# Two parts of x in one 512-column matmul: a float32 decoder trunk on one NeuronCore

## The chip, the cores and the metric

One core of one Trainium2 chip. The metric is the device time of one execution in microseconds (us), the median of three runs. TensorE (PE; its weight loads are shown as PEld), VectorE (DVE), ScalarE (ACT), GpSimd (POOL) and SyncE (SP) each work through a list of their own, in order, and wait for one another on semaphores.

## The reference

Two layers on 256 tokens of width 2048, all in float32:

```
h = rmsnorm(x, norm_mix[l])
x = x + (even_mixer if l == 0 else odd_mixer)(h)
h = rmsnorm(x, norm_ffn[l])
up = h @ w_up;  g, u = split(up)                 # 2 x 5632 columns
x = x + (silu(causal_dwconv(g, conv_w)) * u) @ w_down
...
return rmsnorm(x, norm_final)
```

The even mixer (layer 0) makes q, k, v, a and gate in one projection. Eight heads attend with three dilated windows; beside them a * sigmoid(gate) goes through a causal convolution of width 31, a LayerNorm and a swish. Both go through one output projection, the attention's 1024 rows and then the convolution's. The odd mixer (layer 1) is forgetting attention with 16 heads.

## The kernel before

**Split products.** Weights and activations are each split into two float32r parts whose sum is exact: hi (the rounded value) and lo (the rest). A product is hi·hi + hi·lo + lo·hi. The kernel reads 408 MB of weights once, each in panels of 512 output columns. `stream` (lines 79 to 98) brings 1 MB (four contraction tiles of 128 rows) into `raw` and splits it in two pieces of 128 x 1024: ACT casts `whi` (line 95), DVE subtracts `wlo` (line 96). There are three `raw` buffers and four of each part, so a cast waits until PE is done with the piece four before.

**`panel_b`** (lines 100 to 112) makes a feature-major product. For each of the panel's four feature tiles m it has one PSUM bank of 512 float32 columns, of which the 256 tokens fill the lower half, and for each contraction tile it issues three matmuls of 256 columns: whi with x's hi (line 109), whi with x's lo (line 110), wlo with x's hi (line 111). The weight is the stationary operand, so `whi` is loaded twice. I call these three a triple, and a matmul with its weight load a pass. There are five such banks. `panel_a` (lines 119 to 127) makes a token-major product: x is stationary, and the weight's 512 columns move, so all its passes are 512 columns wide (lines 115 to 117). It serves v in both layers and the last projection (names `acc_v`, `acc_d` of layer 1, `acc_e`).

**Who uses panel_b:** a and gate (`ag`, four panels), q and k of both layers, both output projections (`oa` for the attention's rows, `ob` for the convolution's, `oc` in layer 1), the forget gates (`fl`), the FFN's up projection (`g` and `u`, 11 panels each per layer) and layer 0's down projection (`d`). DVE evicts each bank with one instruction, mostly a multiplication by the norm's row or an addition to x (lines 293, 297, 377, 198, 462, 477, 516).

**What sets the order.** A scheduler writes each engine's list when the program is built, from its own estimate of durations and from priorities: splits of weights stand 400 steps ahead of their place, and the convolution's steps (`waiting`, lines 299 to 320) 300 behind it; a few of them are handed out behind each split (`pace`). What is left is handed out after `oa`'s second panel, and then comes `layer_norm` (lines 405 to 428), whose result y is `ob`'s moving operand: without it `ob` can't start. On the chip the lists are fixed.

Of the kernel before, what the change touches and what calls it, by code (L numbers as in the profile page):

```python
# [41 lines left out]
def trunk(ctx, tc, a):  # L42
# [25 lines left out]
    # work that may wait, traced a little at a time behind the weights' pieces  # L68
# [10 lines left out]
    def stream(src_of, nk, width, name, dk=4, room=None):  # L79
        """The split parts of a weight's panel, a few contraction tiles at a time."""  # L80
# [56 lines left out]
    xT = keep.tile([P, KT, T], F32, name="xT")  # L137
    xs_hi = keep.tile([P, KT, T], F32R, name="xs_hi")
    xs_lo = keep.tile([P, KT, T], F32R, name="xs_lo")
    xhi = lambda kt: xs_hi[:, kt, :]  # L140
    xlo = lambda kt: xs_lo[:, kt, :]
# [15 lines left out]
    def along_free(r, name):  # L157
        """A column per token [128, 2] as a row [128, T], the same on each partition."""
# [9 lines left out]
    def rstd_from(parts, n, name):  # L168
        """From partial sums [128, T] per partition: a column [128 tokens, 2] and a row [128, T]."""
# [21 lines left out]
    def finish_x(kt, gcol, ssq, name):  # L191
        """x's feature tile kt is complete: scaled split copy, and its squares."""
# [14 lines left out]
    ROWS = ((0, 0, P), (1, P, T))     # query tile, its columns in a head's scores, and its keys  # L207
# [34 lines left out]
    def weigh_v(pt, vt, h, yhi, ylo, kt, name):  # L242
# [4 lines left out]
        S.copy(yhi[:, kt, :], y[:, :T])  # L247
        V.tensor_tensor(out=ylo[:, kt, :], in0=y[:, :T], in1=yhi.bitcast(F32)[:, kt, :], op=ALU.subtract)

    # =====================================================================  # L250
    # Layer 0 mixer: dilated attention and Conformer convolution
    # =====================================================================
    with ExitStack() as ph:
# [15 lines left out]
        S.activation(dummy, ones[:, 0:1], AF.Copy)   # brings the activation table while the first loads run  # L269

        # Conformer branch: a and gate columns side by side, then the convolution
        def ag_gemm(i, dk=4):
            srcs = cols(w_in, 6 + i)
            if i > 0:
                return panel_b(srcs, xhi, xlo, list(range(KT)), f"ag{i}", order=(2, 3, 0, 1))
# [12 lines left out]
            return panel_b(first, xhi, xlo, list(range(KT)), "ag0", order=(2, 3, 0, 1), dk=2)  # L288
# [49 lines left out]
        # rotary tables, four heads' 32 rotated dims on the partitions  # L338
# [58 lines left out]
        for hg in range(2):  # L397
            va = panel_a(cols(w_in, 4 + hg), xhi, xlo, list(range(KT)), f"v{hg}")
# [313 lines left out]
```

## Time and profile before

| | us |
|---|---|
| median of 3 runs (2290.03 to 2291.7) | 2290.95 |
| span of the profiled execution, first to last instruction | 2289.1 |
| PE busy (its matmuls; weight loads 2182.5) | 2264.5 |
| DVE busy | 1411.4 |
| ACT busy | 1052.7 |

The page gives the profiled execution's span and no other time of its own; the median stands 1.85 us above that span, which is what lies around it. A busy matmul includes its pipelined fill and drain, so matmuls overlap, and their durations don't add up to time: what one costs is the distance from its start to the next one's.

### The profile page before, as it was taken

To read this page: it belongs to the slowest core of one execution; us is meant where nothing else is said; L and a number is where in the kernel's file an instruction comes from. 1 tells how busy PE (TensorE), PEld (TensorE's weight loads), DVE (VectorE), ACT (ScalarE), POOL (GpSimd) and SP (SyncE) were. 2 spreads that over 40 slices of the span, in tenths; PEclk is the share of its full clock that TensorE was granted. 3 is DMA by queue.
4 is the path that set the end of the run, shared out by engine and by line. 5 is a ranking of instruction groups with operands and counts; after the bars stand their busy time and mean duration, and the time that the engine had idled before them with its cause. 6 is when DMAs were issued, how large, how long until landed. Compare 5 with 4: busy or idle time off the path is not lost.

```text
span 2289.1 us, 40415 instructions
## 1 busy us (share of the span) xinstructions
PE 2264.5 (99%) x17214; PEld 2182.5 (95%) x17214; DVE 1411.4 (62%) x2096; ACT 1052.7 (46%) x1378; POOL 46.1 (2%) x77
## 2 busy tenths in 40 slices
PE   8999999999999999999999999999999999999997
PEld 7999999999999999999989988999999988999986
DVE  6999986666644566565554445556565544565644
ACT  6567665444433344444443444454444433444433
POOL 2000000000000000000010000000000000000001
PEclk9999999999999999999999999999999999999999
DMA  6554455555555555555544544555555555555553
GB/s 228 191 184 165 168 181 184 185 184 181 183 186 187 183 182 182 183 183 186 180 166 148 184 150 164 177 176 184 185 183 184 196 190 188 182 184 184 184 186 126
DMA packets 60260, 412.51 MB, mean 180 GB/s; under 512 B 7232, under 2 KB 7936, under 8 KB 11696
## 3 DMA queue, kind: packets, MB, share of 16 engines
q1 hardware_dynamic: 59328, 408.62, 50.5%
q8 instruction: 134, 2.20, 0.4%
q10 hardware_dynamic: 144, 1.05, 0.1%
q14 instruction: 46, 0.38, 0.0%
q0 software_dynamic: 608, 0.26, 0.0%
HBM read 407.75 MB, written 2.10 MB: 179 GB/s over the span
## 4 chain that ended last, share of the span: by engine, by line
PE 98%; DVE 1%; ACT 1%; DMA 0%; issue 0%; SPq 0%; ACTq 0%
PE acc_g L111 7%; PE acc_g L110 7%; PE acc_g L109 7%; PE acc_u L111 7%; PE acc_u L109 7%; PE acc_u L110 7%; PE acc_d L109 4%; PE acc_d L110 4%; PE acc_d L111 4%; PE acc_q L111 2%; PE acc_k L109 2%; PE acc_k L110 2%; PE acc_k L111 2%; PE acc_q L109 2%; PE acc_q L110 2%; PE acc_v L116 2%
## 5 line engine op out<-in xcount | busy, mean ns | idle before, releaser
L110 PE MATMUL acc_g<-xs_lo,whi_g 128*128 128x256 f32 x1408 | 397.6, 283 | 0.0
L109 PE MATMUL acc_g<-xs_hi,whi_g 128*128 128x256 f32 x1408 | 397.6, 283 | 0.0
L111 PE MATMUL acc_u<-xs_hi,wlo_u 128*128 128x256 f32 x1408 | 397.6, 283 | 0.0
L110 PE MATMUL acc_u<-xs_lo,whi_u 128*128 128x256 f32 x1408 | 397.6, 283 | 0.0
L111 PE MATMUL acc_g<-xs_hi,wlo_g 128*128 128x256 f32 x1408 | 395.6, 283 | 0.0
L109 PE MATMUL acc_u<-xs_hi,whi_u 128*128 128x256 f32 x1408 | 394.9, 283 | 0.0
L96 DVE TENSOR_TENSOR wlo_g<-raw_g,whi_g 128x1024 fp32r<-128x1024 f32 x176 | 215.4, 1224 | 194.6 <-ACT whi_g L95 192.9
L95 ACT CAST whi_u<-raw_u 128x1024 fp32r<-128x1024 f32 x176 | 184.7, 1050 | 292.0 <-PE acc_g L110 160.4
L95 ACT CAST whi_g<-raw_g 128x1024 fp32r<-128x1024 f32 x176 | 184.5, 1048 | 279.6 <-PE acc_u L110 118.9
L96 DVE TENSOR_TENSOR wlo_u<-raw_u,whi_u 128x1024 fp32r<-128x1024 f32 x176 | 215.0, 1222 | 117.1 <-ACT whi_u L95 117.1
L96 DVE TENSOR_TENSOR wlo_d<-raw_d,whi_d 128x1024 fp32r<-128x1024 f32 x136 | 166.6, 1225 | 179.1 <-ACT whi_d L95 179.1
L109 PEld LDWEIGHTS acc_g<-xs_hi,whi_g 128*128 128x128 f32 x1408 | 269.2, 191 | 0.1
L110 PEld LDWEIGHTS acc_u<-xs_lo,whi_u 128*128 128x128 f32 x1408 | 269.2, 191 | 0.0
L111 PEld LDWEIGHTS acc_u<-xs_hi,wlo_u 128*128 128x128 f32 x1408 | 269.2, 191 | 0.0
L110 PEld LDWEIGHTS acc_g<-xs_lo,whi_g 128*128 128x128 f32 x1408 | 269.2, 191 | 0.0
L111 PEld LDWEIGHTS acc_g<-xs_hi,wlo_g 128*128 128x128 f32 x1408 | 267.7, 191 | 0.1
L109 PEld LDWEIGHTS acc_u<-xs_hi,whi_u 128*128 128x128 f32 x1408 | 267.7, 191 | 0.0
L95 ACT CAST whi_d<-raw_d 128x1024 fp32r<-128x1024 f32 x136 | 142.9, 1051 | 223.0 <-PE acc_d L110 127.7
L110 PE MATMUL acc_d<-hl,whi_d 128*128 128x256 f32 x704 | 197.7, 281 | 0.0
L109 PE MATMUL acc_d<-hh,whi_d 128*128 128x256 f32 x704 | 197.7, 281 | 0.0
L111 PE MATMUL acc_d<-hh,wlo_d 128*128 128x256 f32 x704 | 196.8, 281 | 0.0
L109 PEld LDWEIGHTS acc_d<-hh,whi_d 128*128 128x128 f32 x704 | 132.5, 188 | 0.0
(298 smaller groups left out, 5032.4 us busy)
## 6 DMA issues: line engine op xcount, KB each, us to landing
raw_g<-in_ffn_w_up SPq DMA_DIRECT2D x88, 1024.0 KB, 4.8
raw_u<-in_ffn_w_up SPq DMA_DIRECT2D x88, 1024.0 KB, 4.8
raw_d<-in_ffn_w_down SPq DMA_DIRECT2D x68, 1024.0 KB, 4.8
raw_q<-in_od_w_in SPq DMA_DIRECT2D x16, 1024.0 KB, 4.8
raw_k<-in_od_w_in SPq DMA_DIRECT2D x16, 1024.0 KB, 4.8
raw_v<-in_od_w_in SPq DMA_DIRECT2D x16, 1024.0 KB, 4.9
raw_oc<-in_od_w_out SPq DMA_DIRECT2D x16, 1024.0 KB, 4.8
raw_e<-in_ffn_w_down SPq DMA_DIRECT2D x16, 1024.0 KB, 4.8
```

Of the source, the lines that this page charges most:

```text
L95: S.copy(hi, rv[:, h:h + half, :])
L96: last = V.tensor_tensor(out=lo, in0=rv[:, h:h + half, :], in1=hi.bitcast(F32), op=ALU.subtract)
L109: PE.matmul(o, hi[:, j, ms], xhi(kt), start=k == 0, stop=False)
L110: PE.matmul(o, hi[:, j, ms], xlo(kt), start=False, stop=False)
L111: PE.matmul(o, lo[:, j, ms], xhi(kt), start=False, stop=k == len(kts) - 1)
L116: PE.matmul(o, xh, lo, start=False, stop=False)
```

## The change

x's two parts are stored side by side, `xs[P, KT, 2, T]`, and so are the mixers' outputs (`y2`) and the FFN's hidden values (`hp`). In `panel_b` the first matmul now takes hi and lo together as 512 columns and writes the whole bank: whi·hi in the lower half, whi·lo in the upper half. The second, wlo·hi, adds 256 columns to the lower half. At eviction the halves are added: `whole` copies the upper half on ACT and adds the lower half on DVE; `add_x` makes two DVE additions. The norm's factor is then multiplied in a separate, wider DVE instruction. `panel_a` computes as before. Comments went too.

```diff
-    def panel_b(src_of, xhi, xlo, kts, name, order=(0, 1, 2, 3), dk=4, spare=()):
+    def panel_b(src_of, x2, kts, name, order=(0, 1, 2, 3), dk=4):
...
-                    o, kt = acc[m][:, :T], kts[k]
-                    PE.matmul(o, hi[:, j, ms], xhi(kt), start=k == 0, stop=False)
-                    PE.matmul(o, hi[:, j, ms], xlo(kt), start=False, stop=False)
-                    PE.matmul(o, lo[:, j, ms], xhi(kt), start=False, stop=k == len(kts) - 1)
+                    x = x2(kts[k])
+                    PE.matmul(acc[m], hi[:, j, ms], x.rearrange("p a t -> p (a t)"), start=k == 0, stop=False)
+                    PE.matmul(acc[m][:, :T], lo[:, j, ms], x[:, 0, :], start=False, stop=k == len(kts) - 1)
         return acc
+    def whole(out, acc, name):
+        half = wk.tile([P, T], F32, tag="half", name=f"half_{name}", bufs=3)
+        S.copy(half, acc[:, T:])
+        out = half if out is None else out
+        V.tensor_tensor(out=out, in0=acc[:, :T], in1=half, op=ALU.add)
+        return out
...
-            V.tensor_tensor(out=xT[:, 4 * i + m, :], in0=acc[m][:, :T], in1=xT[:, 4 * i + m, :], op=ALU.add)
+            x = xT[:, 4 * i + m, :]
+            V.tensor_tensor(out=x, in0=acc[m][:, T:], in1=x, op=ALU.add)
+            V.tensor_tensor(out=x, in0=acc[m][:, :T], in1=x, op=ALU.add)
...
+            rb2 = rb.unsqueeze(1).broadcast_to([P, 2, T])
+            ab = glu[:, 2 * i:2 * i + 2, KW - 1:]
             for j in range(2):
-                V.tensor_tensor(out=sg[:, j, :], in0=acc[2 + j][:, :T], in1=rb, op=ALU.mult)
+                whole(sg[:, j, :], acc[2 + j], f"g{i}{j}")
+            for j in range(2):
+                whole(ab[:, j, :], acc[j], f"a{i}{j}")
+            V.tensor_tensor(out=sg, in0=sg, in1=rb2, op=ALU.mult)
             S.activation(sg, sg, AF.Sigmoid)
-            V.tensor_tensor(out=sg, in0=sg, in1=rb.unsqueeze(1).broadcast_to([P, 2, T]), op=ALU.mult)
-            for j in range(2):
-                V.tensor_tensor(out=glu[:, 2 * i + j, KW - 1:], in0=acc[j][:, :T], in1=sg[:, j, :], op=ALU.mult)
+            V.tensor_tensor(out=sg, in0=sg, in1=rb2, op=ALU.mult)
+            V.tensor_tensor(out=ab, in0=ab, in1=sg, op=ALU.mult)
...
-                V.tensor_tensor(out=full[:, m, :], in0=acc[m][:, :T], in1=r, op=ALU.mult)
+                whole(full[:, m, :], acc[m], f"{name}{m}")
+            V.tensor_tensor(out=full, in0=full, in1=r.unsqueeze(1).broadcast_to([P, 4, T]), op=ALU.mult)
...
-                        V.tensor_tensor(out=gp[:, m, 2:], in0=acc[m][:, :T], in1=rb, op=ALU.mult)
+                        whole(gp[:, m, 2:], acc[m], f"g{nm}{m}")
+                    rb4 = rb.unsqueeze(1).broadcast_to([P, 4, T])
+                    V.tensor_tensor(out=gp[:, :, 2:], in0=gp[:, :, 2:], in1=rb4, op=ALU.mult)
...
-                        V.tensor_tensor(out=cv[:, m, :], in0=acc[m][:, :T], in1=cv[:, m, :], op=ALU.mult)
+                        h = cv[:, m, :]
+                        V.tensor_tensor(out=h, in0=whole(None, acc[m], f"u{nm}{m}"), in1=h, op=ALU.mult)
```

The scheduler writes new lists. Three places follow; numbers at the end of a name are the program's own.

**DVE in layer 0, the last attention softmax** (`e1`: heads 4 to 7). `L221`, now `L229`, is the row maximum of a head's scores, `nm_e1` its result and `den_e1` the softmax's sum; `wlo_v1_6` is the split of v's second panel from contraction tile 6 on, `wlo_oa0_4` that of the output projection's first panel; `cacc` is the convolution. Before:

```order
L221 ISA pt_e13_2526,nm_e1_2521<-s_e13_2542,mask_1272 128x256
L221 ISA nm_e1_2521 128x1
L312 TENSOR_TENSOR cacc_84<-cacc_84,pr_3_4_2805 128x512
L96 TENSOR_TENSOR wlo_v1_6_2843<-raw_v1_4_2821,whi_v1_6_2842 128x1024
L223 TENSOR_SCALAR nm_e1_2521<-nm_e1_2521 128x8
L304 SCALAR_TENSOR_TENSOR cacc_84<-glu_83,cw_85,cacc_84 128x256 x2
L96 TENSOR_TENSOR wlo_v1_8_2866<-raw_v1_8_2863,whi_v1_8_2865 128x1024
```

and with the change:

```order
L229 ISA pt_e13_2088,nm_e1_2083<-s_e13_2104,mask_1055 128x256
L229 ISA nm_e1_2083 128x1
L316 SCALAR_TENSOR_TENSOR cacc_83<-glu_82,cw_84,cacc_83 128x256 x3
L96 TENSOR_TENSOR wlo_oa0_4_2590<-raw_oa0_4_2587,whi_oa0_4_2589 128x1024
L231 TENSOR_SCALAR nm_e1_2083<-nm_e1_2083 128x8
L324 TENSOR_TENSOR cacc_83<-cacc_83,pr_3_4_2367 128x512
L316 SCALAR_TENSOR_TENSOR cacc_83<-glu_82,cw_84,cacc_83 128x256 x2
L96 TENSOR_TENSOR wlo_oa0_6_2617<-raw_oa0_4_2587,whi_oa0_6_2616 128x1024
L316 SCALAR_TENSOR_TENSOR cacc_83<-glu_82,cw_84,cacc_83 128x256 x4
L236 RECIPROCAL den_e1_2084<-den_e1_2084 128x8
```

The maxima moved from ahead of v1's fourth split to behind its last one and among `oa0`'s.

**DVE in layer 0, the LayerNorm's first sum** (`csum1`, over channels 512 to 1023). `acc_oa1` is the output projection's second panel, `wlo_oa2` the third's split. Before:

```order
L304 SCALAR_TENSOR_TENSOR cacc_84<-glu_83,cw_85,cacc_84 128x256 x4
L96 TENSOR_TENSOR wlo_oa2_0_3340<-raw_oa2_0_3337,whi_oa2_0_3339 128x1024
L413 TENSOR_REDUCE csum1_3263<-cacc_84 128x256
L96 TENSOR_TENSOR wlo_oa2_2_3368<-raw_oa2_0_3337,whi_oa2_2_3367 128x1024
L198 TENSOR_TENSOR xT_77<-acc_oa1_0_3113,xT_77 128x256
```

and with the change:

```order
L316 SCALAR_TENSOR_TENSOR cacc_83<-glu_82,cw_84,cacc_83 128x256 x4
L205 TENSOR_TENSOR xT_77<-acc_oa1_0_2647,xT_77 128x256
L205 TENSOR_TENSOR xT_77<-acc_oa1_1_2648,xT_77 128x256
L425 TENSOR_REDUCE csum1_2769<-cacc_83 128x256
L206 TENSOR_TENSOR xT_77<-acc_oa1_0_2647,xT_77 128x256
L205 TENSOR_TENSOR xT_77<-acc_oa1_2_2649,xT_77 128x256
L206 TENSOR_TENSOR xT_77<-acc_oa1_1_2648,xT_77 128x256
L96 TENSOR_TENSOR wlo_oa2_0_2846<-raw_oa2_0_2843,whi_oa2_0_2845 128x1024
```

The sum now stands behind two additions that read the second panel's result, and the third panel's first split behind the sum.

**ACT at a panel's end in the FFN** (layer 0, from panel `u0_4` to `g0_5`), with the change:

```order
L95 CAST whi_g0_5_4_5563<-raw_g0_5_4_5561 128x1024
L116 COPY half_u0_40_5491<-acc_u0_4_0_5318 128x256
L116 COPY half_u0_41_5497<-acc_u0_4_1_5319 128x256
L116 COPY half_u0_42_5503<-acc_u0_4_2_5320 128x256
L95 CAST whi_g0_5_6_5583<-raw_g0_5_4_5561 128x1024
L491 CAST hp0_4_5490<-cv0_4_5290 128x256
L116 COPY half_u0_43_5509<-acc_u0_4_3_5321 128x256
```

Before, the four copies weren't there; the casts stood in the same order.

## Rows read from the trace of the kernel before

**Rows 1.** The page: busy time of each engine, and the chain's shares by engine.

```profile
PE 2264.5 (99%) x17214; PEld 2182.5 (95%) x17214; DVE 1411.4 (62%) x2096; ACT 1052.7 (46%) x1378; POOL 46.1 (2%) x77
...
PE 98%; DVE 1%; ACT 1%; DMA 0%; issue 0%; SPq 0%; ACTq 0%
```

**Rows 2.** Instructions by tile in three stretches: min/median/max ns, first and last start.

```profile
L109 PE MATMUL acc_u<-xs_hi,whi_u x64: 283/283/283, 606.5 to 629.2; 128*128 128x256 f32 x64
...
L109 PE MATMUL acc_d<-hh,whi_d x384: 279/281/285, 629.5 to 765.9; 128*128 128x256 f32 x192
...
L116 PE MATMUL acc_d<-wlo_d,hh x164: 392/392/392, 1823.1 to 1935.0; 128*128 128x512 f32 x164
```

**Rows 3.** Timeline of PE where widths change: start, duration (us), instruction.

```profile
1163.11 0.28 PE L111 MATMUL acc_k<-xs_hi,wlo_k 128*128 128x256 f32 x1
1163.23 0.40 PE L115 MATMUL acc_v<-whi_v,xs_hi 128*128 128x512 f32 x1
...
1427.76 0.39 PE L117 MATMUL acc_v<-whi_v,xs_lo 128*128 128x512 f32 x1
1427.99 0.28 PE L109 MATMUL acc_oc<-yhi,whi_oc 128*128 128x256 f32 x1
```

**Rows 4.** Line 109, whole span: each panel kind's count of triples.

```profile
L109 PE MATMUL acc_g<-xs_hi,whi_g x1408: 278/283/287, 352.2 to 2142.5; 128*128 128x256 f32 x176
...
L109 PE MATMUL acc_u<-xs_hi,whi_u x1408: 280/283/287, 376.1 to 2165.5; 128*128 128x256 f32 x176
...
L109 PE MATMUL acc_d<-hh,whi_d x704: 279/281/285, 629.5 to 1110.2; 128*128 128x256 f32 x176
...
L109 PE MATMUL acc_q<-xs_hi,whi_q x384: 278/283/288, 108.9 to 1374.9; 128*128 128x256 f32 x192
...
L109 PE MATMUL acc_k<-xs_hi,whi_k x384: 281/283/468, 155.0 to 1397.9; 128*128 128x256 f32 x192
...
L109 PE MATMUL acc_oc<-yhi,whi_oc x256: 277/281/286, 1428.0 to 1522.4; 128*128 128x256 f32 x128
...
L109 PE MATMUL acc_ob<-yhi,whi_ob x128: 277/281/384, 305.6 to 351.8; 128*128 128x256 f32 x128
```

**Rows 5.** Busy time in two stretches: window, length, then each engine's.

```profile
57.00:286.00 229.00, 229.00 (x1716) 220.04 (x1716) 212.14 (x395) 147.57 (x257) 0.00 (x0) 1.00 0.51 177
400.00:650.00 250.00, 250.00 (x2088) 250.00 (x2087) 153.46 (x216) 103.79 (x116) 0.53 (x5) 1.00 0.51 182
```

**Rows 6.** Groups by line, 40 to 312 us: busy us, mean ns of one.

```profile
L304 DVE SCALAR_TENSOR_TENSOR cacc<-glu,cw,cacc 128x256 f32<-128x256 f32 x160 | 69.9, 478 | 0.2
L312 DVE TENSOR_TENSOR cacc<-cacc,pr 128x512 f32<-128x512 f32 x40 | 27.3, 685 | 0.3
...
L198 DVE TENSOR_TENSOR xT<-acc_oa,xT 128x256 f32<-128x256 f32 x16 | 6.1, 419 | 0.0
...
L420 DVE TENSOR_TENSOR cacc<-cacc,mus 128x1024 f32<-128x1024 f32 x2 | 2.4, 1218 | 0.0
...
L311 ACT ACTIVATE pr<-glu,cw 128x256 f32<-128x256 f32 x80 | 36.1, 501 | 13.6 <-DVE cacc L312 12.2 <-DVE glu L297 1.2
...
L227 ACT ACTIVATE pt_e<-pt_e,nm_e 128x256 f32<-128x256 f32 x8 | 4.0, 495 | 0.0
```

**Rows 7.** Layer 0's mixer: single rows of timeline and tile views.

```profile
244.38 1.23 DVE L96 TENSOR_TENSOR wlo_v<-raw_v,whi_v 128x1024 fp32r<-128x1024 f32 x1 [0.79 <-ACT whi_v L95]
...
254.62 0.72 PE L109 MATMUL acc_oa<-yhi,whi_oa 128*128 128x256 f32 x4
...
L413 DVE TENSOR_REDUCE csum<-cacc x2: 2015/2024/2032, 172.6 to 277.3; 128x256 f32<-128x1024 f32 x2
...
307.11 0.39 PE L110 MATMUL acc_ob<-ylo,whi_ob 128*128 128x256 f32 x1
```

**Rows 8.** Busy time near the start; the column behind POOL is PE's granted clock.

```profile
11.00:21.00 10.00, 8.05 (x66) 7.64 (x64) 9.34 (x14) 9.95 (x23) 6.31 (x6) 1.00 0.63 237
21.00:28.00 7.00, 5.66 (x27) 5.66 (x28) 4.88 (x5) 3.47 (x8) 5.59 (x4) 0.51 0.49 142
```

**Rows 9.** PE's waits, the last projection's row: total us, times, longest.

```profile
PE acc_e L115 <- DVE cv L477: 0.9, 1, 0.9
```

More of the change, by code (lines that the diff above doesn't have):

```diff
@@ L98, in stream @@
                 yield list(range(c + h, c + h + half)), hi, lo
-    def panel_b(src_of, xhi, xlo, kts, name, order=(0, 1, 2, 3), dk=4, spare=()):
-        acc = {m: misc(f"acc_{name}_{m}") if m in spare else pacc.tile([P, 512], F32, tag="acc", name=f"acc_{name}_{m}")
-               for m in order}
+    def panel_b(src_of, x2, kts, name, order=(0, 1, 2, 3), dk=4):
+        acc = {m: pacc.tile([P, 512], F32, tag="acc", name=f"acc_{name}_{m}") for m in order}
         for ks, hi, lo in stream(src_of, len(kts), P * len(order), name, dk):
@@ L137, in trunk @@
     xT = keep.tile([P, KT, T], F32, name="xT")
[L138 to L141, printed above, removed]
+    xs = keep.tile([P, KT, 2, T], F32R, name="xs")
+    x2 = lambda kt: xs[:, kt, :, :]
     def rsqrt_cols(ps, scale, name, n=2):
@@ L274, in ag_gemm @@
             if i > 0:
-                return panel_b(srcs, xhi, xlo, list(range(KT)), f"ag{i}", order=(2, 3, 0, 1))
+                return panel_b(srcs, x2, list(range(KT)), f"ag{i}", order=(2, 3, 0, 1))
             def first(c, n):
@@ L367, in trunk @@
         yp = ph.enter_context(tc.tile_pool(name="y0", bufs=1))
-        yhi = yp.tile([P, KT, T], F32R, name="yhi")
-        ylo = yp.tile([P, KT, T], F32R, name="ylo")
+        y2 = yp.tile([P, KT, 2, T], F32R, name="y2")
         swap = [(i + 16) % 32 for i in range(32)]
         def qk_panel(c0, r, name):
-            acc = panel_b(cols(w_in, c0 // 512), xhi, xlo, list(range(KT)), name)
+            acc = panel_b(cols(w_in, c0 // 512), x2, list(range(KT)), name)
             full = mx.tile([P, 4, T], F32, tag=name[0], name=name, bufs=2)
@@ L397, in trunk @@
         for hg in range(2):
-            va = panel_a(cols(w_in, 4 + hg), xhi, xlo, list(range(KT)), f"v{hg}")
+            va = panel_a(cols(w_in, 4 + hg), x2, list(range(KT)), f"v{hg}")
             vt = mx.tile([P, 4, T], F32, tag="q", name=f"vt{hg}", bufs=2).rearrange("p (t k) c -> p t (k c)", t=2)
@@ L426, in layer_norm @@
                 S.activation(cacc[:, c, :], cacc[:, c, :], AF.Silu, scale=vcol[:, 72 + c:73 + c], bias=vcol[:, 80 + c:81 + c])
-                S.copy(yhi[:, 8 + c, :], cacc[:, c, :])
-                V.tensor_tensor(out=ylo[:, 8 + c, :], in0=cacc[:, c, :], in1=yhi.bitcast(F32)[:, 8 + c, :], op=ALU.subtract)
+                S.copy(y2[:, 8 + c, 0, :], cacc[:, c, :])
+                V.tensor_tensor(out=y2[:, 8 + c, 1, :], in0=cacc[:, c, :], in1=y2.bitcast(F32)[:, 8 + c, 0, :], op=ALU.subtract)
         pace[0] = P_O
         for i in range(4):
-            acc = panel_b(cols(w_out, i), lambda k: yhi[:, k, :], lambda k: ylo[:, k, :], list(range(8)), f"oa{i}")
+            acc = panel_b(cols(w_out, i), lambda k: y2[:, k, :, :], list(range(8)), f"oa{i}")
             add_x(acc, i)
@@ L441, in trunk @@
         for i in range(4):
-            acc = panel_b(cols(w_out, i, k0=1024), lambda k: yhi[:, k, :], lambda k: ylo[:, k, :],
-                          list(range(8, 16)), f"ob{i}")
+            acc = panel_b(cols(w_out, i, k0=1024), lambda k: y2[:, k, :, :], list(range(8, 16)), f"ob{i}")
             add_x(acc, i, then=lambda kt: finish_x(kt, 32 + kt, ssq, "f0"))
@@ L453, in ffn @@
             for gi, (p0, p1) in enumerate(UP_GROUPS):
-                hh, hl = [], []
+                h2 = []
                 for p in range(p0, p1):
                     nm = f"{l}_{p}"
-                    acc = panel_b(cols(w_up, p), xhi, xlo, list(range(KT)), f"g{nm}")
+                    acc = panel_b(cols(w_up, p), x2, list(range(KT)), f"g{nm}")
                     gp = fp.tile([P, 4, T + 2], F32, tag="gp", name=f"gp{nm}", bufs=2)
@@ L471, in ffn, with down0 @@
                     S.activation(cv, cv, AF.Silu)
[L472 to L475 removed]
+                    V.tensor_tensor(out=cv, in0=cv, in1=rb4, op=ALU.mult)
+                    acc = panel_b(cols(w_up, FF // 512 + p), x2, list(range(KT)), f"u{nm}")
+                    hp = fp.tile([P, 4, 2, T], F32R, tag="hp", name=f"hp{nm}", bufs=6)
                     for m in range(4):
[L477 to L484 removed]
+                        h = cv[:, m, :]
+                        V.tensor_tensor(out=h, in0=whole(None, acc[m], f"u{nm}{m}"), in1=h, op=ALU.mult)
+                        copies.append(S.copy(hp[:, m, 0, :], h))
+                        V.tensor_tensor(out=hp[:, m, 1, :], in0=h, in1=hp.bitcast(F32)[:, m, 0, :], op=ALU.subtract)
+                    h2.append(hp)
+                g2 = lambda k: h2[k // 4][:, k % 4, :, :]
+                down(gi, w_dn, 512 * p0, list(range(4 * (p1 - p0))), g2, fp)
     ssq1 = new_ssq("m1")
[L488 removed]
+    def down0(gi, w_dn, k0, kts, g2, fp):
         for i in range(4):
[L490 removed]
+            acc = panel_b(cols(w_dn, i, k0=k0), g2, kts, f"d0{gi}{i}")
             add_x(acc, i, then=(lambda kt: finish_x(kt, 16 + kt, ssq1, "m1")) if gi == 1 else None)
@@ L505, in trunk @@
         G.dma_start(out=bf[P - NHC:P, :], in_=a["od_b_f"].rearrange("l h -> h l"))
-        yhi = mx.tile([P, KT, T], F32R, name="yhi1")
-        ylo = mx.tile([P, KT, T], F32R, name="ylo1")
+        y2 = mx.tile([P, KT, 2, T], F32R, name="y21")
         rcol, rb = rstd_from([ssq1], D, "m1")
@@ L512, in qk1 @@
         def qk1(c0, r, name):
-            acc = panel_b(cols(w_in, c0 // 512), xhi, xlo, list(range(KT)), name)
+            acc = panel_b(cols(w_in, c0 // 512), x2, list(range(KT)), name)
             full = mx.tile([P, 4, T], F32, tag=name[0] + "1", name=name, bufs=2)
             for m in range(4):
-                V.tensor_tensor(out=full[:, m, :], in0=acc[m][:, :T], in1=r, op=ALU.mult)
+                whole(full[:, m, :], acc[m], f"{name}{m}")
+            V.tensor_tensor(out=full, in0=full, in1=r.unsqueeze(1).broadcast_to([P, 4, T]), op=ALU.mult)
             return full
         def forget_gates():
-            acc = panel_b(lambda c, n: a["od_w_f"], xhi, xlo, list(range(KT)), "fl", order=(0,))
+            acc = panel_b(lambda c, n: a["od_w_f"], x2, list(range(KT)), "fl", order=(0,))
             g0 = slice(96, P)
@@ L555, in trunk @@
             pts = softmax_t(mx, qf, kf, mask, f"o{hg}", bias=(fq, fk))
-            va = panel_a(cols(w_in, 8 + hg), xhi, xlo, list(range(KT)), f"v1{hg}")
+            va = panel_a(cols(w_in, 8 + hg), x2, list(range(KT)), f"v1{hg}")
             vt = mx.tile([P, 2, 512], F32, tag="vt1", name=f"vt1{hg}")
@@ L560, in trunk @@
             for m in range(4):
-                weigh_v(pts[m], vt, m, yhi, ylo, 4 * hg + m, f"o{hg}{m}")
+                weigh_v(pts[m], vt, m, y2, 4 * hg + m, f"o{hg}{m}")
         ssq2 = new_ssq("f1")
         for i in range(4):
-            acc = panel_b(cols(w_out, i), lambda k: yhi[:, k, :], lambda k: ylo[:, k, :], list(range(KT)), f"oc{i}")
+            acc = panel_b(cols(w_out, i), lambda k: y2[:, k, :, :], list(range(KT)), f"oc{i}")
             add_x(acc, i, then=lambda kt: finish_x(kt, 48 + kt, ssq2, "f1"))
```

43 lines of the change are left out of this document (16 added, 27 removed).

## The prediction
> **What bounds the kernel now.** I read the page's busy times and the chain of waits first. PE is busy 99% of the span, and 98% of the chain that ended last is PE [rows 1]: what PE has to do is the time, nearly everywhere. Then I read PE's pace, from the first and last start of a line's instructions in one undisturbed stretch. In a `u` panel, 64 triples start within 606.5 to 629.2 us: 22.7 / 63 = 0.360 us for three 256-column passes, 120 ns each [rows 2]. In layer 0's down projection, 384 triples take 136.4 / 383 = 0.356 us, 118.7 ns a pass. In the 512-column passes of layer 1's down projection, line 116 comes 164 times in 111.9 us: 111.9 / 163 = 0.686 us for three, 228.8 ns a pass. Two narrow passes cost 240 ns, one wide one 229: each pass has a part of some 11 ns that doesn't grow with its columns. That part is what the change can save.
>
> Last I read busy time by stretch, for what covers the rest [rows 5]. In the FFN DVE is busy 153.46 of 250 us (61%) and ACT 42%: there is room. In layer 0's mixer, from 57 to 286 us, DVE is busy 212.14 of 229 us (93%): there it runs beside PE with almost nothing to spare, because the convolution's steps are given to it.
>
> **What the change does to PE.** A triple becomes a wide pass and a narrow one. No stretch of before alternates the two, but the seams between panels show both steps: from a narrow pass to the next, wide one 0.12 us, from a wide one to a narrow one 0.23 us [rows 3], which is what each costs among its own kind. So I price the pair at 228.8 + 120.0 = 348.8 ns against 360, and 228.8 + 118.7 = 347.5 against 356 for the panels whose moving operand isn't `xs`: 11.2 and 8.5 ns saved. The bounds: the dearest pair is one that saves nothing (768 columns cost what they cost); the cheapest has the narrow pass at half of the wide one, 228.8 × 1.5 = 343.2 ns, saving 16.8 and 12.8. I take the middle, for the seams show it.
>
> Which triples count? Those behind layer 0's LayerNorm, where PE is the bound: `g` and `u` 1408 each, of `q` and `k` the 256 each of layer 1 (four of six panels), together 3328; `d` 704, `oc` 256, `ob` 128, together 1088 [rows 4]. The saving is 3328 × 11.2 = 37.3 plus 1088 × 8.5 = 9.2 ns: **46.5 us**; by the bounds 0 to 69.8. The triples ahead of it (`ag`, `q`, `k` of layer 0, `oa`) save some 6 us of PE, which are lost in the next step.
>
> **What it does to layer 0's mixer.** DVE gets more work there. Each of four `ag` panels had four 256-wide instructions and one 512-wide; now four and three: 2 × 0.685 = 1.4 us more. Each of four `q` and `k` panels gets one 1024-wide multiplication, 1.22 us. Each of `oa`'s 16 banks gets a second addition, 0.42 us [rows 6]. That is 5.5 + 4.9 + 6.7 = 17 us, as much as the 16.9 us that DVE was idle in those 229. ACT's 32 copies (about 0.4 us each) fit into its 81 idle us.
>
> The order makes it worse. The last softmax's maxima now stand behind v's last split, with the convolution between. From that split's end to the negated maxima DVE has one addition and two more among three 512-wide ones (3 × 0.68), ten convolution steps (10 × 0.437, busy over count), three splits (3 × 1.22) and four heads' maxima (about 0.9 each): 13.7 us. Then ACT takes the exponentials (16 of up to 0.5 us with their sums, 5 us) and DVE the reciprocal, behind which stand 16 convolution steps and four 512-wide additions, 9.7 us, ahead of the first y: 29 us in all. The last v split ended at 245.6 us [rows 7]; with PE 5 us earlier I put it at 241, so `oa` begins at about 270 instead of 254.6. PE, done with v at some 249, has nothing to do meanwhile. From there, `csum1` waits behind two additions of `oa`'s second panel, and DVE has ten more additions on the way to y than before (4 us). Before, 29.8 us lay between `csum1` and the first `ob` matmul that needs y's lo part (277.3 to 307.1). I expect that matmul at 321, 14 us later.
>
> PE's idle time has a price of its own. In the start, PE was busy 8.05 of 10 us, and its granted clock was then 0.51 of full for 7 us [rows 8]: the lower level, 1.2 GHz. Two waits of over 5 us, ahead of `oa` and of `ob`, should do the same; the first is hidden in the wait for y, the second costs half of 6.8 us, 3.4. Sum for this part: **+17 us**. Bounds: +1 (DVE takes all of it into its idle time, and `oa` isn't late) to +30 (the 15 us of `oa` and the 17 us of work add up).
>
> **Edits at nothing, and their cover.** In the FFN each bank now needs an ACT copy and a DVE addition before it is free. Of five banks one is free when a panel ends, so the next panel's second feature tile needs the first bank 0.7 us after the old panel's last piece ended, 2.8 us after its own result was done. In ACT's list the cast ahead of the copies (1.05 us) starts when the piece before is done, so the bank is free after a cast, a split and an addition, about 2.6 us after the last piece began, against 3.5 needed: 0.9 us to spare, and as much for the others. If the cover is gone, each of some 60 seams costs PE the excess. DVE's extra instructions there (per `g` and `u` pair 5 of 0.42 us and one of 1.22, beside 45 us of PE) leave it under 75%. Layer 1's mixer has the same evictions and DVE half busy. DMA moves what it moved. Where the last projection opens its own banks, PE waited 0.9 us for the last eviction [rows 9]; that eviction is one copy and one addition longer: **+1 us**.
>
> The sum, against the profiled execution's span of 2289.1: 2289.1 − 46.5 + 17 + 1 = 2260.6. The median stands 1.85 us above that span, so I forecast **2262 us**.
>
> **The rivals.**
> A. *Layer 0 isn't delayed.* DVE's 16.9 idle us take the added 17, and the softmax's late place is paid by waits that were there anyway. Then the 6 us ahead count too: 2290.95 − 46.5 − 6 + 2 = 2240. For it: the order is made by a scheduler that weighs PE. Against it: 93% busy with every gap a wait for a cast, and `ob` already waited for y.
> B. *The pair costs what the triple cost*, in every `panel_b`: the 11 ns belong to the columns, not to the pass, or come back as a wait for the second weight. The kernel keeps the added evictions and is slower: 2290.95 + 18 = 2309. It decides the sign once a triple saves less than 18 / 4416 = 4 ns. For it: no stretch shows the alternation. Against it: both seams. The Trainium skill (TensorE: Matmul & The Clock Gate, Back-to-back issue gap) puts the fixed part of a warm pass at 2.5 ns beside its columns' time. By that rule the change would save an estimated 4416 × 2.5 = 11 us and end at 2298, slower; the rows here, 120 and 228.8 ns, disagree with it.
> C. *The seams bite.* The bank's release comes one split (1.22 us) later than I place it; 0.9 us are covered, and 0.3 × 60 = 18 us are added: 2280.
> D. *The pair is cheap*, as by the lower bound: 2262 − 23 = 2239.
>
> **How the numbers follow.** I give my forecast 0.64, A 0.13, B 0.08, C 0.09, D 0.06. A measurement of this kernel can tell about 0.2%, 4.6 us, from no change. The range takes in A, D and C, and the forecast with its layer 0 part up to +30 and a pair some ns dearer: **2238 to 2284**; the forecast's own cases lie in 2250 to 2276. Faster: the forecast, A, D and nearly all of C, 0.88; within 0.2%: 0.04, from C and the dear end of the forecast; slower: B, 0.08.
>
> **What would show it.** Right: in a `u` panel the 64 pairs start 0.347 to 0.351 us apart; from 400 us on PE never waits; the first `ob` matmul with y stands near 321 us, with PE idle and its clock at half around 250 to 270 and again before it; from there to the end the time is some 46 us shorter. Wrong, step by step: a pair near 0.360 (B) or 0.343 (D); `ob` starting before 307 (A); PE waiting at the start of every FFN panel for line 118 or ACT's copies (C). A kernel that is slower with pairs at 0.349 would say that I have overlooked a wait.

## The result and the profile after

The changed kernel takes **2268.77 us** (median of 4 runs, 2266.76 to 2269.37) beside 2291.07 for the kernel before on the same chip: a ratio of 0.9902 with a 95% interval of 0.9888 to 0.9916. That is faster by 22 us where 29 had been forecast, and inside the range. The profiled execution took 2266.76 us, its span 2265.0 against 2289.1. Two single disturbed executions, 3873 us in `last_u_triple` and 4662 us in `groups_of_4`, are left out of the medians below.

The page's busy times and the chain's shares, to be read beside [rows 1]:

```profile
PE 2226.5 (98%) x12142; PEld 1915.6 (85%) x12142; DVE 1510.7 (67%) x2307; ACT 1131.3 (50%) x1619; POOL 45.5 (2%) x77
...
PE 97%; DVE 1%; ACT 1%; DMA 0%; issue 0%; SPq 0%; ACTq 0%; DVEq 0%
```

PE is still the bound and has 5072 passes fewer; PEld, busy 95% before, is at 85%. DVE has 211 instructions more.

Instructions by tile in one `u` panel and in layer 0's first down projection, as in [rows 2] (min/median/max ns, first and last start):

```profile
L109 PE MATMUL acc_u<-xs,whi_u x64: 387/395/403, 613.1 to 635.1; 128*128 128x512 f32 x64
L110 PE MATMUL acc_u<-xs,wlo_u x64: 274/280/285, 613.3 to 635.3; 128*128 128x256 f32 x64
...
L109 PE MATMUL acc_d<-hp,whi_d x384: 387/396/401, 635.5 to 770.0; 128*128 128x512 f32 x192
```

From the first wide pass of `u` to the first of `d` lie 22.4 us for 64 pairs, 350 ns each; over ten panels of layer 0 (411.2 to 635.5 us, 640 pairs) it is 350.5, where the same ten panels took 360.0 before (399.1 to 629.5). `d` takes 134.5 / 383 = 351.2.

PE's four longest waits, to be read beside [rows 9] (total us, times, longest):

```profile
PE acc_ag L109 <- ACT whi_ag L95: 8.2, 2, 7.1
PE tp_e L246 <- ACT pt_e L241: 6.3, 1, 6.3
PE acc_ob L109 <- DVE y L440: 4.2, 2, 3.9
PE acc_e L122 <- DVE half_u L118: 3.3, 1, 3.3
```

The first stands at the start, where the kernel before had 9.2. The next two are new: the second softmax of layer 0 ahead of `oa`, and the convolution's y ahead of `ob`. The fourth, for the last `u` panel's eviction ahead of the last projection, was 0.9 before. Of the shorter ones, 2.0 us for `oa`'s splits and 1.2 within the softmax's transposes are new too. Between 323 and 2138 us PE waits for nothing.

Busy time in five stretches, the first two as in [rows 5] (window, length, PE, PEld, DVE, ACT, POOL, then PE's granted clock):

```profile
57.00:286.00 229.00, 221.52 (x1193) 190.62 (x1193) 214.82 (x405) 152.76 (x283) 0.00 (x0) 0.97 0.47 166
400.00:650.00 250.00, 250.00 (x1429) 217.95 (x1428) 173.07 (x253) 121.78 (x164) 0.53 (x5) 1.00 0.53 190
...
247.00:262.00 15.00, 9.10 (x33) 7.30 (x34) 14.58 (x33) 13.32 (x43) 0.00 (x0) 0.54 0.24 87
319.00:323.00 4.00, 3.75 (x15) 2.83 (x14) 3.40 (x8) 3.18 (x10) 0.00 (x0) 0.57 0.79 283
2142.00:2146.00 4.00, 4.00 (x12) 3.16 (x11) 1.05 (x3) 1.90 (x3) 0.00 (x0) 0.57 0.61 254
```

In the FFN DVE went from 153 to 173 us of 250 and still leaves room. The last three stretches begin within or just behind the waits ahead of `oa`, `ob` and the last projection, and in each the clock was granted at half for a while.

Layer 0's mixer in the timeline (start, duration, instruction, idle time before it); DVE's rows of the second softmax and of the first y:

```profile
246.70 0.17 DVE L231 TENSOR_SCALAR nm_e<-nm_e 128x8 f32<-128x8 f32 x1
...
250.88 0.20 DVE L236 RECIPROCAL den_e<-den_e 128x8 f32<-128x8 f32 x1
...
259.13 0.41 DVE L256 TENSOR_TENSOR y<-y_e,y 128x256 fp32r<-128x256 f32 x1
```

And PE's:

```profile
245.03 0.39 PE L124 MATMUL acc_v<-whi_v,xs 128*128 128x512 f32 x1
251.73 2.47 PE L246 MATMUL tp_e<-cst,pt_e 128*128 128x128 f32 x9 [6.32 <-ACT pt_e L241]
...
261.04 0.64 PE L109 MATMUL acc_oa<-y,whi_oa 128*128 128x512 f32 x1
...
318.23 0.47 PE L109 MATMUL acc_ob<-y,whi_ob 128*128 128x512 f32 x1 [3.93 <-DVE y L440]
```

PE is done with v at 245 and finds the second softmax unfinished: its maxima end at 246.7, and PE stands until 251.7. `oa` begins at 261.0, where [rows 7] had 254.62; `ob` begins at 318.2 after another wait.

Where the time went, from first matmuls in the traces (us; the column "mixer" is the run `l0_triples` below, "both" is `l0_and_last_u_triples`):

| first matmul of | before | after | mixer | both |
|---|---|---|---|---|
| `oa` | 254.6 | 261.0 | 253.9 | 254.7 |
| `ob` | 305.6 | 318.2 | 306.4 | 307.2 |
| first `g`, layer 0 | 352.2 | 365.5 | 351.8 | 352.7 |
| layer 1's first `q` | 1110.5 | 1106.8 | 1093.1 | 1094.0 |
| first `g`, layer 1 | 1522.7 | 1509.9 | 1496.3 | 1497.2 |
| last projection | 2166.9 | 2141.7 | 2128.1 | 2127.2 |
| span | 2289.1 | 2265.0 | 2252.4 | 2249.2 |

The change loses 13.3 us up to the first `g`, wins 38.5 from there to the last projection, and loses 1.1 in that projection: 24.1 in the span.

### The profile page after: what moved, and what is told of

It is laid out like the page before. It is cut to its first block, busy times and chain, and to the rows that moved or that the text cites. A ratio compares the mean times of both kernels' runs of the same rounds, so it can differ in the third digit from the quotient of the medians.

```text
span 2265.0 us, 30815 instructions
## 1 busy us (share of the span) xinstructions
PE 2226.5 (98%) x12142; PEld 1915.6 (85%) x12142; DVE 1510.7 (67%) x2307; ACT 1131.3 (50%) x1619; POOL 45.5 (2%) x77
## 4 chain that ended last, share of the span: by engine, by line
PE 97%; DVE 1%; ACT 1%; DMA 0%; issue 0%; SPq 0%; ACTq 0%; DVEq 0%
PE acc_g L109 15%; PE acc_u L109 14%; PE acc_g L110 7%; PE acc_u L110 7%; PE acc_d L109 7%; PE acc_q L109 4%; PE acc_k L109 4%; PE acc_d L110 4%; PE acc_oc L109 3%; PE acc_ag L109 2%; PE acc_q L110 2%; PE acc_k L110 2%; PE acc_v L122 2%; PE acc_v L123 2%; PE acc_d L122 2%; PE acc_d L124 2%
## 5 line engine op out<-in xcount | busy, mean ns | idle before, releaser
L109 PE MATMUL acc_g<-xs,whi_g 128*128 128x512 f32 x1408 | 493.1, 397 | 0.0
L109 PE MATMUL acc_u<-xs,whi_u 128*128 128x512 f32 x1408 | 481.9, 395 | 0.0
L110 PE MATMUL acc_g<-xs,wlo_g 128*128 128x256 f32 x1408 | 388.8, 280 | 0.0
L110 PE MATMUL acc_u<-xs,wlo_u 128*128 128x256 f32 x1408 | 370.0, 279 | 0.0
L109 PEld LDWEIGHTS acc_g<-xs,whi_g 128*128 128x128 f32 x1408 | 262.6, 188 | 60.7
L109 PEld LDWEIGHTS acc_u<-xs,whi_u 128*128 128x128 f32 x1408 | 260.1, 188 | 52.7
L110 PEld LDWEIGHTS acc_u<-xs,wlo_u 128*128 128x128 f32 x1408 | 265.0, 188 | 9.0
L110 PEld LDWEIGHTS acc_g<-xs,wlo_g 128*128 128x128 f32 x1408 | 265.6, 189 | 3.0 <-DVE wlo_g L96 0.2
L109 PE MATMUL acc_d<-hp,whi_d 128*128 128x512 f32 x704 | 245.2, 394 | 0.0
L110 PE MATMUL acc_d<-hp,wlo_d 128*128 128x256 f32 x704 | 194.4, 283 | 0.0
L109 PEld LDWEIGHTS acc_d<-hp,whi_d 128*128 128x128 f32 x704 | 131.3, 188 | 28.8
```

The source lines that it names most:

```text
L109: PE.matmul(acc[m], hi[:, j, ms], x.rearrange("p a t -> p (a t)"), start=k == 0, stop=False)
L110: PE.matmul(acc[m][:, :T], lo[:, j, ms], x[:, 0, :], start=False, stop=k == len(kts) - 1)
```

## The experiments

**Layer 0's mixer, as a square of two parts.** Each run takes triples and single-instruction evictions back in some panels; all else is the change. `panel_b` gets a switch:

```diff
+                    if tri:
+                        o = acc[m][:, :T]
+                        PE.matmul(o, hi[:, j, ms], x[:, 0, :], start=k == 0, stop=False)
+                        PE.matmul(o, hi[:, j, ms], x[:, 1, :], start=False, stop=False)
+                        PE.matmul(o, lo[:, j, ms], x[:, 0, :], start=False, stop=k == len(kts) - 1)
+                        continue
```

`l0_triples`: ag, q, k and oa.

> All panels of layer 0's mixer ahead of its LayerNorm (ag, q, k, oa) go back to triples and single-instruction evictions; everything behind keeps the pairs. Theory (DVE work and its order in the mixer cost the change some 13 us there): v begins near 204 and oa near 255 us as before, the first ob matmul that needs y lo near 307, the first FFN panel near 351.5 instead of 365.5, and the time is 2268.8 - 14 = 2255 (2252 to 2258). Rival (the mixer is paced by something else, such as the clock or the loads, and the delay stays): 2268. Second rival (the 6 us that pairs save PE ahead of the LayerNorm were of use): a part of the 14 is lost and the time is about 2261.

`oa_triples`: oa alone.

> Only oa goes back to triples with one addition; ag, q and k keep pairs and their longer evictions, and with them the late place of the second softmax. Theory (both parts count: the added work and late softmax ahead of oa, and oa's additions on the way to y): oa still begins near 261, the first ob matmul with y lo comes 4 to 6 us earlier than 318, and the time is about 2263. Rival 1 (only the order ahead of oa counts): 2268. Rival 2 (only oa's 16 additions count): 2255.

`agqk_triples`: ag, q and k alone.

> ag, q and k go back to triples with single-instruction evictions, which puts the second softmax back between v's splits; oa keeps pairs and two additions. Theory (both parts count): oa begins near 254.6, the first ob matmul with y lo near 312 instead of 307 or 318, time about 2260. Rival 1 (only the order ahead of oa counts): 2255. Rival 2 (only oa's additions count): 2268. With the runs l0_triples and oa_triples this makes a square of two parts.

| triples in | time, us | ratio to before, interval | csum1 starts | `ob` starts |
|---|---|---|---|---|
| none (the change) | 2268.77 | 0.9902, 0.9888 to 0.9916 | 284.1 | 318.2 |
| oa | 2259.4 | 0.9862, 0.9847 to 0.9877 | 284.0 | 312.8 |
| ag, q, k | 2261.07 | 0.9866, 0.985 to 0.9883 | 276.5 | 311.7 |
| ag, q, k, oa | 2253.89 | 0.9838, 0.9823 to 0.9853 | 276.6 | 306.4 |

The first theory holds: the mixer cost 14.9 us, and both parts count. `l0_triples` and `agqk_triples` came where they were expected. `oa_triples` took 2259.4 us, 3.6 below its theory's 2263 and on the way to its second rival's 2255 (only `oa`'s additions count); against that rival stands `agqk_triples`, which keeps these additions and still gains 7.7 us. PE's timeline where `ob` begins, in `l0_triples`:

```profile
306.37 0.50 PE L115 MATMUL acc_ob<-y,whi_ob 128*128 128x512 f32 x1 [1.39 <-DVE y L442]
```

The same row in `agqk_triples`:

```profile
311.66 0.77 PE L115 MATMUL acc_ob<-y,whi_ob 128*128 128x512 f32 x1 [5.66 <-DVE y L442]
```

And the second softmax's transposes ahead of `oa`, in `oa_triples`:

```profile
252.38 2.48 PE L253 MATMUL tp_e<-cst,pt_e 128*128 128x128 f32 x9 [6.32 <-ACT pt_e L248]
```

These are two mechanisms. With pairs in oa alone (`agqk_triples`), `oa` and csum1 stand where they stood before, but `ob` comes 35.1 us behind csum1 instead of 29.8 (`l0_triples`): DVE has oa's second additions on the way to y, and PE waits 5.66 us. With pairs in ag, q and k alone (`oa_triples`) it is the other way: the late softmax makes PE wait 6.32 us ahead of `oa`, and from there on PE is the later one, with only 1.4 us of waiting at `ob`. Whether the late softmax comes from DVE's added work or from its new place in DVE's order was not separated: these runs change both.

**The last projection.** `last_u_triple` takes the triple back in one panel.

```diff
-                    acc = panel_b(cols(w_up, FF // 512 + p), x2, list(range(KT)), f"u{nm}")
+                    acc = panel_b(cols(w_up, FF // 512 + p), x2, list(range(KT)), f"u{nm}", tri=(l, p) == (1, 10))
...
-                        V.tensor_tensor(out=h, in0=whole(None, acc[m], f"u{nm}{m}"), in1=h, op=ALU.mult)
+                        u = acc[m][:, :T] if (l, p) == (1, 10) else whole(None, acc[m], f"u{nm}{m}")
+                        V.tensor_tensor(out=h, in0=u, in1=h, op=ALU.mult)
```

> Only the last u panel (layer 1, panel 10), whose banks the last projection opens anew, goes back to triples and a one-instruction eviction. Theory (PE's wait of 3.3 us ahead of the last projection, and the half clock of 3.4 us that follows it, are due to the longer eviction): the wait falls to about 1 us, no half clock near 2140, the panel itself is 0.6 us longer, and the time falls by 3 to 4 us to about 2265. Rival (the half clock comes at that place for another reason): the wait falls but the clock stays, and the time falls by under 2.5 us.

It took 2264.23 us (0.9881, 0.9864 to 0.9897). The wait is back to 0.92 us, and from the second pass on those behind it start 0.23 us apart, where the changed kernel had 0.43 us until 2145.3:

```profile
2141.83 0.47 PE L128 MATMUL acc_e<-whi_e,hp 128*128 128x512 f32 x1 [0.92 <-DVE cv L497]
2142.14 0.39 PE L129 MATMUL acc_e<-wlo_e,hp 128*128 128x512 f32 x1
2142.38 0.39 PE L130 MATMUL acc_e<-whi_e,hp 128*128 128x512 f32 x1
```

The interval overlaps that of the change, so the gain rests on the trace: 2.4 us less of waiting, and the projection itself takes 121.7 us instead of 123.3; against that the triples lengthen the panel by an estimated 0.6 us (64 × 9.5 ns). The two spans differ by only 1.5 us (2263.5 against 2265.0), because this execution came to its first `g` 1.8 us later (367.3 against 365.5). Its clock was at half between 304 and 308 us, behind waits of 0.63 and 1.17 us for splits of `oa`'s weights; the changed kernel had the same two waits there and kept the full clock. This execution's row of that stretch, then the changed kernel's:

```profile
304.00:308.00 4.00, 3.71 (x12) 3.23 (x13) 3.36 (x15) 0.20 (x1) 0.00 (x0) 0.57 0.67 238
304.00:308.00 4.00, 3.28 (x19) 2.90 (x20) 3.79 (x15) 0.20 (x1) 0.00 (x0) 1.00 0.54 182
```

**Evictions without the merge.** In `evictions_only` everything is as in the change, save that the wide pass is two narrow ones again.

```diff
-                    PE.matmul(acc[m], hi[:, j, ms], x.rearrange("p a t -> p (a t)"), start=k == 0, stop=False)
+                    PE.matmul(acc[m][:, :T], hi[:, j, ms], x[:, 0, :], start=k == 0, stop=False)
+                    PE.matmul(acc[m][:, T:], hi[:, j, ms], x[:, 1, :], start=False, stop=False)
```

> Nothing is merged: three 256-column passes as before, but the pass of the weight's first part on x's lo part goes to the upper half of the bank, so every eviction and every order is that of the change. Theory (the saving is the merged pass alone; the evictions cost about 13 us in layer 0's mixer and 3.5 us at the last projection and nothing elsewhere): a triple stays at 0.356 to 0.360 us and the time is 2291 + 17 = 2308 (2303 to 2312). Rival 1 (evictions cost something at each of some 60 FFN seams too): 2320 or more. Rival 2 (evictions are covered when PE isn't faster): 2291 to 2296.

It took 2311.1 us (1.009, 1.0077 to 1.0103): slower than before by 20 us, and nearly all of it is where the theory put it. The first `g` starts at 369.0 (before: 352.2), and from there to the last projection it takes 1816.5 us (before: 1814.7), though 2.3 us more of waiting at the end are in that. The FFN's seams cost nothing that shows: the twelve panels from the first `g` to the first `d` take 277.3 us in both. From the first `g` to the end the change takes 40.8 us less than this kernel: that is what merging is worth behind the mixer.

**What a pass costs.** `narrow_split` cuts the narrow pass of `g` and `u` in two; `lo_columns` widens it to 384 columns in `g` and to 512 in `u`, which adds the second parts' product.

```diff
-                    PE.matmul(acc[m][:, :T], lo[:, j, ms], x[:, 0, :], start=False, stop=k == len(kts) - 1)
+                    cuts = (0, P, T) if name[0] in "gu" else (0, T)
+                    for c0, c1 in zip(cuts, cuts[1:]):
+                        PE.matmul(acc[m][:, c0:c1], lo[:, j, ms], x[:, 0, c0:c1], start=False, stop=c1 == T and k == len(kts) - 1)
```

> In the g and u panels alone the narrow pass is cut into two of 128 columns, the same columns in all: 2816 passes and weight loads more. Theory of the prediction (a pass has a part of some 11 ns that doesn't grow with its columns): the three passes take about 351 + 11 = 362 ns, the time is 2269 + 31 = 2300. Rival 1 (cost goes by columns alone, what the change saved is something else): 351 ns, 2269. Rival 2 (a pass can't be shorter than its weight load takes, which would put the floor near 116 ns): 233 + 2 x 116 = 466 ns, 2269 + 2816 x 0.116 = 2595.

> Starts from the changed kernel. The second pass of a pair takes more of x's columns in two kinds of panel, so lo x lo terms are added that the reference's split leaves out: 384 instead of 256 columns in g, 512 in u; passes and weight loads stay as many as they are. Read against each other: in the changed kernel the narrow pass takes 116.5 ns, the wide one 233. Theory after narrow_split (a pass costs its columns at 0.455 ns each, with hardly a fixed part, but not less than some 113 ns): the second pass takes 384 x 0.455 = 175 ns in g and 233 in u; time 2269 + 1408 x (0.058 + 0.1165) = 2514. Rival (columns at 1/2.4 ns and a fixed part of 20 ns that the narrow pass hides): 180 ns in g, 233 in u; 2521.

They took 2566.43 and 2499.88 us (ratios 1.1201 and 1.0911, 1.1179 to 1.1222 and 1.088 to 1.0943). One `u` panel of `narrow_split`, by tile:

```profile
L112 PE MATMUL acc_u<-xs,wlo_u x128: 220/273/277, 688.4 to 717.2; 128*128 128x128 f32 x128
L109 PE MATMUL acc_u<-xs,whi_u x64: 393/448/450, 688.1 to 716.9; 128*128 128x512 f32 x64
```

A `g` and a `u` panel of `lo_columns`:

```profile
L109 PE MATMUL acc_g<-xs,whi_g x64: 389/398/398, 645.2 to 671.1; 128*128 128x512 f32 x64
L111 PE MATMUL acc_g<-xs,wlo_g x64: 333/338/338, 645.4 to 671.4; 128*128 128x384 f32 x64
...
L109 PE MATMUL acc_u<-xs,whi_u x64: 389/389/398, 671.6 to 700.2; 128*128 128x512 f32 x64
```

A wide pass and two of 128 columns take 28.8 / 63 = 457 ns. With 229 to 233 for the wide one, a 128-column pass costs 112 to 114 ns, hardly less than one of 256. So rival 2 of `narrow_split` holds in kind: there is a floor per pass, near 113 ns (its 116 ns and 2595 us were a little high). The prediction's premise, a constant of 11 ns beside the columns, does not reach down to this width: with (228.8 − 120) / 256 = 0.425 ns per column it gives an estimated 65 ns for 128 columns.

In the other kernel 896 columns in two passes take 25.9 / 63 = 411 ns, 1024 take 28.6 / 63 = 454, beside 350.5 for the pair's 768: 0.44 to 0.46 ns per column. Both texts on record for `lo_columns` missed its time: the theory (columns at 0.455 ns with hardly a fixed part) said 2514 us and the rival 2521. The prediction's premise would have given pairs of 403 and 458 ns, against 349 for the pair as it is, and 2268.8 + 1408 × (0.054 + 0.109) = 2498 us. That is nearly the time measured, but its misses on the two pairs, 8 ns too little and 4 too much, partly cancel. From 256 to 512 columns these runs don't tell a fixed part per pass from a cost by columns alone.

The Trainium skill (TensorE: Matmul & The Clock Gate, LDWEIGHTS) gives a weight load as its columns over 1.2, an estimated 107 ns for 128 columns. The trace agrees as far as the distance between loads goes: in the panel of `narrow_split` matmuls start as little as 57 ns apart, but weight loads nowhere under 108, though each is drawn as 187 to 192 ns long. Two starts of loads there:

```profile
690.59 0.19 PEld L109 LDWEIGHTS acc_u<-xs,whi_u 128*128 128x128 f32 x1
690.70 0.42 PEld L112 LDWEIGHTS acc_u<-xs,wlo_u 128*128 128x128 f32 x2
```

That the floor is the weight's load is argued from this, and from PEld, busy all 250 us of an FFN stretch whose passes were all narrow [rows 5] and 217.95 in the changed kernel; no run here took a load away. What merging saves is then this: narrow passes in a row, 120 ns each, take 0.469 ns per column, a pair 0.456.

**Both losses undone.** `l0_and_last_u_triples` joins `l0_triples` and `last_u_triple`.

> Triples in layer 0's mixer (ag, q, k, oa) and in the last u panel, pairs everywhere else: both measured losses undone at once. Theory (they are independent): 2253.9 - 4 = 2250 (2247 to 2252). Rival (the last projection's gain depends on what goes before it): 2254.

It took 2250.71 us (0.9821, 0.9807 to 0.9835), as the theory said.

**The order of the passes.** `grouped_pairs` starts from that kernel and moves the narrow passes of a piece behind its wide ones, per feature tile.

```diff
-                    PE.matmul(acc[m][:, :T], lo[:, j, ms], x[:, 0, :], start=False, stop=k == len(kts) - 1)
+                for j, k in enumerate(ks):
+                    if not tri:
+                        x = x2(kts[k])
+                        PE.matmul(acc[m][:, :T], lo[:, j, ms], x[:, 0, :], start=False, stop=k == len(kts) - 1)
```

> As the run l0_and_last_u_triples, but in each panel the two wide passes of a piece stand ahead of its two narrow ones instead of alternating. In the profile of the changed kernel a narrow pass after a narrow one took 118 ns and a wide one after a wide one 231, against 116.5 and 233 to 234 in alternation: theory (grouping is worth 1 to 2 ns per pair): 4416 x 1.5 = 6.6 us, so 2243 (2241 to 2247). Rival (the step between shapes costs nothing by itself): same as that run, 2250.

It took **2244.21 us** (0.9796, 0.9784 to 0.9809), the fastest version found. Its first down projection, by tile:

```profile
L115 PE MATMUL acc_d<-hp,whi_d x384: 387/392/398, 620.9 to 754.4; 128*128 128x512 f32 x192
```

That of `l0_and_last_u_triples`:

```profile
L115 PE MATMUL acc_d<-hp,whi_d x384: 387/396/401, 622.6 to 757.1; 128*128 128x512 f32 x192
```

From this panel's first pass to the next panel's first it is 134.0 instead of 134.9 us (from 620.9 to 754.9, and from 622.6 to 757.5). The gain is real (2243.9 to 2245.6 us in five executions against 2249.0 to 2251.0); its reason is not the one given, as the next runs show. `groups_of_4` and `groups_of_8` make the groups longer, over two and over four feature tiles:

```diff
+            for m0 in range(0, len(order), 2):
...
+                for m, ms in ms4:
+                    for j, k in enumerate(ks):
+                        PE.matmul(acc[m], hi[:, j, ms], x2(kts[k]).rearrange("p a t -> p (a t)"), start=k == 0, stop=False)
+                for m, ms in ms4:
+                    for j, k in enumerate(ks):
+                        PE.matmul(acc[m][:, :T], lo[:, j, ms], x2(kts[k])[:, 0, :], start=False, stop=k == len(kts) - 1)
```

> As grouped_pairs (two wide, then two narrow passes; 2244.2), but over two feature tiles at a time: four wide, then four narrow. Theory (each change between a wide and a narrow pass costs time: one change less per pair gave 2250.7 - 2244.2 = 6.5 us, or 1.5 ns per pair): half a change less per pair gives another 3 us, 2241. Rival 1 (what grouping gained was not the changes): 2244. Rival 2 (the later end of the first banks makes PE wait at the panels' seams): over 2248.

> Eight wide, then eight narrow passes per piece, over all four feature tiles. Theory as for groups_of_4: another 1.6 us less than that run, 2239.5. Rival 1: 2244. Rival 2 (the first bank is complete 1 us later and the next panel opens it 0.2 us earlier, so that PE waits at the seams of some 60 panels): over 2250, with waits for the evictions' additions in the list of waits.

They took 2252.36 and 2251.71 us (both 0.9826): the gain is gone. The theory misses, and so does the rival that names these times, for there are no new waits at the seams. A cost for changing the accumulator's bank would have explained all four; `bank_each_pair` tests it by alternating over the feature tiles.

```diff
+                steps = [(m, j, k) for j, k in enumerate(ks) for m in order]
```

> As l0_and_last_u_triples (2250.7): wide and narrow passes alternate, but the accumulator's bank changes after each pair instead of after two. Theory formed after groups_of_4 and groups_of_8 (a change between wide and narrow costs 1.5 ns, a change of the bank that the pass writes about 5.3 ns: it fits all four runs, for groups_of_4 and groups_of_8 change the bank twice as often per pair as grouped_pairs): half a change more per pair, 4416 x 2.65 = 11.7 us, so 2262 (2258 to 2265). Rival 1 (the bank does not matter, the long groups were slower for another reason): 2251. Rival 2 (it gains, as the same bank isn't written four times running): under 2247.

It took 2250.6 us (0.982, 0.9806 to 0.9833): changing the bank after each pair costs nothing that shows, and that theory fell too. Over the ten panels ahead of `d` a pair takes 348.4 ns in `grouped_pairs` and 349.4 to 350.5 in the four other orders, in `d` 348.8 against 350.7 to 351.2. It isn't cheaper everywhere: from `oc`'s first pass to layer 1's first `g`, `grouped_pairs` takes 94.3 us, strict alternation 93.7. Why two wide and two narrow passes per bank are 1 to 2 ns per pair cheaper in those panels stays open.

## Why the prediction was right, and where its sizes were off

- **What bounds the kernel** was read rightly: PE, except in layer 0's mixer, where DVE decides. `evictions_only` and the square show both halves.
- **The saving of 46.5 us** is the term that was mis-sized most. The pairs take 350.5 ns where 348.8 was forecast, and 351.2 where 347.5 was: 9.5 and about 5 ns saved instead of 11.2 and 8.5. That is 3328 × 9.5 + 1088 × 5 = 37 us, some 0.6 of it in `ob`, ahead of the first `g`. Without the longer wait at its end (2.4 us) the stretch from the first `g` to the last projection won 40.9 us; some 3 us of what it won above that lie in layer 1's mixer ahead of `oc`, and there `evictions_only`, where nothing is merged, is 1.8 us shorter than before too. The step that failed is "the seams show it": the timeline's 0.12 and 0.23 us are too coarse for a term of 2 ns in 349, and in the alternation a wide pass takes 231 to 234 ns, more than the 228.8 of its own kind, and a narrow one 116 to 117, less than 120.
- **Its explanation**, a part of some 11 ns in each pass that doesn't grow with its columns, fails at 128 columns (`narrow_split`: 2300 us expected from it, 2566 measured); between 256 and 512 no run refutes it or shows it. It did no harm because the price was put together from whole passes of the widths that the change uses.
- **Layer 0's mixer at +17 us**: the first `g` is 13.3 us late, undoing it wins 14.9, and the evictions alone cost 16.8. The mechanism is as forecast step by step: maxima 11.3 us behind v's last split (13.7 forecast), the reciprocal 4 later, the first y lo 8.3 behind that (9.7). But `oa` came at 261.0, not 270: that split ended at 235.4 where 241 had been put, and the way to y was 5 us shorter. PE started v 10.6 us earlier than before (193.0 against 203.7), not 5: `evictions_only`, where nothing is merged, starts it 4.2 us earlier (199.5), so only the rest is the pairs of ag, q and k. `ob` at 318.2 (321 forecast) came close by luck in part: `oa` was 9 us earlier than forecast, and the way from `oa` to `ob` took 57.2 us where the forecast left 51. In it are 5.4 us for oa's additions (4 forecast). The half clock behind that wait lasted 3.4 us, not 6.8.
- **The last projection's banks at +1 us** were 2.4 us of wait and 1.1 us of slower passes: the half clock that was counted ahead of `ob` was forgotten here.
- **Edits at nothing** held. PE waits at none of the FFN's seams, and `evictions_only`, at the old pace, shows no cost there either. Rival C is out, as are A (the mixer was delayed), B (the pair is 9.5 ns cheaper) and D.

The forecast was 6.8 us low, with errors that partly cancel: 5.6 on the saving and 2.5 at the last projection, less 3.7 on the mixer, and the rest in how the profiled execution stands to the median (it was 2 us below).

## What to carry to other kernels

Merging two narrow matmuls on the same weight pays where TensorE is the bound and its bank's eviction has cover; where VectorE paces the stage, each extra eviction instruction is paid for, so such a change belongs only in the panels that have the cover: that alone was worth 18 us of 2269 here. Look at the few places where an eviction ends a stage, for there it is not hidden, and the clock can fall behind the wait. Price a pass from whole passes of the same width in the same order, and read the pace over a hundred of them, not from single starts.

## What the runs showed of the hardware

- Passes with a weight load of their own cost 0.44 to 0.47 ns per column from 256 to 512 columns, and 112 to 114 ns at 128 columns.
- In `narrow_split`'s `u` panel weight loads of 128 columns start at least 108 ns apart, matmuls as little as 57 ns.
- Four orders of the same wide and narrow passes gave 2250.6 to 2252.4 us, and a fifth gave 2244.2.
- In the runs here, PE's granted clock was at half after waits of 3.3, 3.9, 5.7 and 6.3 us, and stayed full after waits of 1.4 us ahead of `ob` and 0.9 us ahead of the last projection. Around the two waits of 0.63 and 1.17 us among `oa`'s passes it stayed full in the changed kernel and was at half for 3.4 us in `last_u_triple`, `narrow_split` and `lo_columns`: waits this short are no assurance of the full clock. Behind the 5.7 us, in `agqk_triples`, it was 0.50 from 311 to 316 us:

```profile
311.00:316.00 5.00, 4.34 (x13) 3.76 (x14) 3.13 (x9) 4.36 (x12) 0.00 (x0) 0.50 0.25 103
```
